# Gathered rows written first, VectorE for the last weight splits, norm factors on GpSimd, weights in blocks

## The chip, the cores and the metric

One core of one Trainium2 chip runs the whole program. The metric is the device time in microseconds, from launch to end; the median of three runs stands for a kernel. The core has TensorE (PE; PEld is its weight load), VectorE (DVE), ScalarE (ACT), GpSimd (POOL) and SyncE (SP). SP issues most transfers; GpSimd issues the gathers and scatters and most of the expert weights.

## The reference

A one-layer encoder block on 512 tokens plus 16 meta tokens, 1024 channels, all float32. Two attentions run side by side on the same normed input, their outputs are gated and merged, and a mixture of experts follows in which each expert picks its own 66 tokens:

```python
u = rms_norm(h, g_mix[layer])
z = jnp.einsum('bld,df->blf', u, w_in[layer])
qa, ka, va, qb, kb, vb, ga, gb = jnp.split(z, cut, axis=-1)
oa = diff_attention(...)                      # 8 heads, two softmaxes each
oa = rms_norm(oa, g_subln[layer]) * (1.0 - lam_init)
qh = axial_rope(rms_norm(qb, g_qnorm[layer]), ...)
kh = axial_rope(rms_norm(kb, g_knorm[layer]), ...)
ob = gqa_attention(qh, kh, vb)                # 8 query heads, 2 key heads
merged = sigmoid(ga) * (oa @ w_branch_a) + sigmoid(gb) * (ob @ w_branch_b)
h = h + merged @ w_out[layer]
un = rms_norm(h, g_ffn[layer])
aff = softmax(un @ w_router)                  # 16 experts
top_aff, top_idx = lax.top_k(swapaxes(aff, 1, 2), 66)
xs = un[top_idx]
y = (silu(xs @ w_gate) * (xs @ w_up)) @ w_down * top_aff
h = h.at[top_idx].add(y)
return rms_norm(h, g_final)[:, N_META:]
```

## The kernel before, in words

**Arithmetic.** float32 products are made of float32r halves: a tile is split into a high half (a ScalarE copy that rounds) and a low half (the difference, on VectorE or GpSimd; `hi_lo`, line 440), and a product is three matmuls: high by high, high by low, low by high.

**Projections.** All weights of the first part are taken as 76 column tiles of 1024 x 128 in a fixed order (`order`, line 514): for each of 8 heads of the first attention q, k, v; then the second attention's tiles mixed with the first gates and branch A; then 8 each of gb, yb (branch B) and wo (output projection). `load_weights` (465) brings a tile in from SP, three buffers deep (wraw); a row of it is 128 numbers, so each partition reads 8 runs of 512 bytes. `split_weights` (477) splits it in two parts; the low half goes to `spare_engine()` (444), which is GpSimd unless its planned queue is over 800 ns ahead. `project` (493) makes 24 matmuls for columns 0 to 255 and 24 for the other 272, splits the next tile meanwhile, and yields after matmuls 6, 12, 18 of each half and after the half's evacuation, so that other work can be put between.

**Order.** `Pace` (126) keeps a planned clock for each engine. TensorE and DMA instructions are issued in program order; ScalarE, VectorE and GpSimd instructions wait in a list and are issued by planned start and by `pace.prio` (lower goes first). The order on each engine is fixed at build time.

**Norm factors.** For the 8 heads of the first attention, the 8 queries and the 2 keys of the second, `add_norm` (739) and `norm` (746) sum squares with matmuls against `sel`, turn the sums so that they stand in 5 columns (tile cols5), and `rsqrt` (453) takes the reciprocal root on VectorE: a bit trick and three Newton steps, 11 instructions. For the heads and keys TensorE then spreads the factors over a row (`tr` of a broadcast column) and VectorE multiplies; for the queries the factors become scale and bias of the softmax (cols).

**Output projection and routing.** For d = 0 to 7 `project` makes wo's block d. `route(d)` (1307) adds it to h2T, splits the sum (hh, hl), squares it, and leaves its matmuls for router logits and square sums in `routed`; the loop of the next block issues one of them after each of its first yields:

```python
for n, _ in enumerate(g):
    if n < todo:
        routed.pop(0)()
```

Before the last block `split_piece(0)` (1266) splits the first quarter of expert 0's gate matrix, low half on GpSimd; quarters 1 and 2 follow after the routing probabilities.

**Rows.** `put_rows(t)` (1362) turns 88 tokens of h2T back into rows (t = 0 to 5; the last has 72 tokens and the 16 meta tokens, hence two transfers), copies them to SBUF, and sends them to acc in DRAM, where the experts' results are added later. When the norm factors rc are known, `send_rows` (1379) lets GpSimd write the factor into 4 more columns, and the same rows go to urow in DRAM (1028 columns), from which the experts gather. Rows 0, 1, 2, 4 and 5 use the three wraw buffers, row 3 one named ys. All of these transfers are issued by SP. Beside them VectorE finds each expert's 66 best tokens in 9 rounds (line 1437); `until(idxu)` (1468) plans for the indices; `gather(e)` (1472) takes a wraw buffer and reads the rows of expert e from urow by an indirect transfer of GpSimd.

**Experts.** 48 matrices of 2 MB stream through a ring of 8 buffers (`ring`, 1200, `load_mat`, 1211); the first (tiles named first, tags xa and xb) and the next seven are loaded by SP while wo and the routing run, the rest by GpSimd when VectorE has released a buffer. Each is split in four pieces by ScalarE (eh) and VectorE (el), and TensorE multiplies. Matrix 7 goes where mg_l was. The last expert's rows are added in SBUF, the final norm is made, and the output is written.

## Time and profile before

| What | Value |
|---|---|
| median of three runs | 1073.41 us (1071.48 to 1073.82) |
| the profiled execution, time | 1074.43 us |
| the profiled execution, span | 1072.7 us, mean granted clock 0.968 |
| PE busy | 969.4 us (90%) |
| DVE busy | 758.2 us (71%) |
| ACT busy | 630.8 us (59%) |
| POOL busy | 338.7 us (32%) |
| first attention, second attention, wo and routing, experts | about 30 to 305, 305 to 582, 670 to 752, 765 to 1045 us |

Every instruction stands under line 199, where the planner issues it, so the groups are told apart by their tiles: wl<-wraw,wh is the low half of a weight tile, cols the 5-column factors, hl the low half of h2T, row the rows, xs the gathered rows, raw the expert weights, eh and el the halves of a piece. Times in a timeline count from the first instruction. "[0.52 <-DVE hl]" behind an instruction means that its engine stood idle for 0.52 us before it, and that an instruction of VectorE that wrote hl ended that.

### The profile page before, as it was taken

Reading aid. Unit: us, or ns where it says so; the run is one execution under the profiler, and the core shown is the slowest. Engines: PE = TensorE matmul, PEld = TensorE weight load, DVE = VectorE, ACT = ScalarE, POOL = GpSimd, SP = SyncE. Lnnn points to the kernel's source line nnn. Section 1 sums busy time; section 2 is a strip of 40 time slices with the busy share of each in tenths; the row PEclk is TensorE's granted clock in tenths of the full one; section 3 lists DMA queues with packets and bytes.
Section 4 is the critical chain, followed back from the end, with each engine's and each line's share of the span. In section 5 each row is a group of like instructions: output and inputs, shape, how many; then the busy total and the mean of one; then the engine's idle time right before and its main releaser. Section 6 shows DMA issues by size and latency. Waiting matters only on the chain.

```text
span 1072.7 us, 18211 instructions
## 1 busy us (share of the span) xinstructions
PE 969.4 (90%) x6835; PEld 836.1 (78%) x6835; DVE 758.2 (71%) x1550; ACT 630.8 (59%) x1297; POOL 338.7 (32%) x306
## 2 busy tenths in 40 slices
PE   4799999999968999999999999985499999999984
PEld 4799998999958989999999999974256666666562
DVE  5367788887785677676656145566389999999885
ACT  5366666665745455555545433334288888888773
POOL 3232322322312322333223234432223333323153
PEclk9899999999989999999999999998699999999997
DMA  8544444443111222222222545915899999999964
GB/s 246 166 126 109 124 122 119 130 126 100 55 51 42 66 62 71 69 56 65 70 60 83 160 157 171 328 73 201 237 301 376 324 381 328 381 342 361 349 182 184
DMA packets 127502, 186.44 MB, mean 174 GB/s; under 512 B 6298, under 2 KB 84263, under 8 KB 127414
## 3 DMA queue, kind: packets, MB, share of 16 engines
q1 hardware_dynamic: 101046, 87.96, 27.5%
q0 software_dynamic: 25760, 95.16, 26.2%
q10 hardware_dynamic: 608, 2.16, 0.7%
q8 instruction: 54, 0.88, 0.3%
q14 instruction: 34, 0.28, 0.1%
HBM read 162.07 MB, written 10.76 MB: 161 GB/s over the span
## 4 chain that ended last, share of the span: by engine, by line
PE 57%; DVE 21%; ACT 9%; DMA 5%; issue 5%; SPq 1%; POOL 1%; POOLq 0%; ACTq 0%; DVEq 0%
PE pz L199 33%; PE psc L199 19%; PE ptr L199 5%; DVE sn L199 4%; DVE cols L199 3%; ACT sn L199 2%; DVE ls L199 2%; DVE pb L199 2%; SPq L199 1%; DVE wtl L199 1%; DMA raw<-in_w_down_dram 1%; DVE hl L199 1%; DVE nmb L199 1%; DVE ql L199 1%; DVE zb L199 1%
## 5 line engine op out<-in xcount | busy, mean ns | idle before, releaser
L199 POOL TENSOR_TENSOR wl<-wraw,wh 128x512 fp32r<-128x512 f32 x139 | 190.6, 1381 | 475.2 <-ACT wh L199 453.1
L199 PE MATMUL pz<-u_h,wh 128*128 128x256 f32 (+1 forms) x832 | 247.2, 297 | 5.4 <-ACT u_h L199 2.3
L199 PE MATMUL pz<-u_h,wl 128*128 128x256 f32 (+1 forms) x832 | 238.6, 287 | 1.1 <-POOL wl L199 1.1
L199 PE MATMUL pz<-u_l,wh 128*128 128x256 f32 (+1 forms) x832 | 238.4, 287 | 0.4 <-DVE u_l L199 0.4
L199 DVE TENSOR_TENSOR el<-raw,eh 128x1024 fp32r<-128x1024 f32 x180 | 214.0, 1229 | 6.0 <-ACT eh L199 4.9
L199 ACT CAST eh<-raw 128x1024 fp32r<-128x1024 f32 x180 | 182.0, 1049 | 23.5 <-PE pz L199 14.9
L199 PEld LDWEIGHTS pz<-u_h,wh 128*128 128x128 f32 x832 | 158.8, 191 | 8.3 <-DVE kbuf L199 2.7
L199 PEld LDWEIGHTS pz<-u_h,wl 128*128 128x128 f32 x832 | 158.5, 190 | 1.3 <-POOL wl L199 1.3
L199 PEld LDWEIGHTS pz<-u_l,wh 128*128 128x128 f32 x832 | 158.8, 191 | 0.6 <-DVE u_l L199 0.6
L199 PE MATMUL psc<-eh,xh 128*66 128x512 f32 (+1 forms) x272 | 105.0, 386 | 2.7 <-ACT hid L199 2.2
L199 ACT CAST wh<-wraw 128x512 fp32r<-128x512 f32 x152 | 91.0, 617 | 24.2 <-PE pz L199 10.9
L199 PE MATMUL psc<-el,xh 128*66 128x512 f32 (+1 forms) x272 | 104.1, 383 | 0.9 <-DVE el L199 0.9
L199 PE MATMUL psc<-eh,xl 128*66 128x512 f32 (+1 forms) x272 | 104.0, 382 | 0.0
L199 DVE TENSOR_TENSOR wtl<-ptr,wth 128x512 fp32r<-128x512 f32 (+1 forms) x72 | 45.9, 637 | 46.7 <-ACT wth L199 46.1
L199 ACT ACTIVATE sn<-sn,nm 128x528 f32<-128x528 f32 x64 | 47.1, 736 | 47.0 <-DVE nm L199 46.4
L199 PE MATMUL pz<-eh,hhl 128*66 128x512 f32 x224 | 70.7, 396 | 0.6 <-DVE hhl L199 0.6
L199 POOL DMA_INDIRECT acc<-ys,idxu x15 | 28.8, 1921 | 119.8 <-ACT ys L199 117.5
L199 ACT CAST wth<-ptr 128x512 fp32r<-128x512 f32 (+1 forms) x72 | 39.0, 542 | 46.0 <-PE ptr L199 45.5
L199 PEld LDWEIGHTS psc<-eh,xh 128*66 128x66 f32 x272 | 37.5, 138 | 25.4 <-ACT hid L199 3.2
L199 PEld LDWEIGHTS psc<-el,xh 128*66 128x66 f32 x272 | 37.3, 137 | 24.4 <-DVE el L199 1.4
L199 PEld LDWEIGHTS psc<-eh,xl 128*66 128x66 f32 x272 | 37.4, 138 | 21.9 <-issue 0.6
L199 DVE CUSTOM_DVE_ANT_0 sn<-psc,biases 128x528 f32<-128x528 f32 x64 | 44.3, 694 | 6.2 <-PE psc L199 6.2
(311 smaller groups left out, 2352.2 us busy)
## 6 DMA issues: line engine op xcount, KB each, us to landing
wraw<-in_w_in_dram SPq DMA_DIRECT2D x52, 512.0 KB
raw<-in_w_gate_dram POOLq DMA_DIRECT2D x13, 2048.0 KB, 18.5
raw<-in_w_down_dram POOLq DMA_DIRECT2D x13, 2048.0 KB, 15.4
raw<-in_w_up_dram POOLq DMA_DIRECT2D x13, 2048.0 KB, 20.4
biases<-in_c_bias_dram SPq DMA_DIRECT2D x8, 1056.0 KB
kbuf<-kbuf SPq DMA_DIRECT2D x32, 132.0 KB
wraw<-in_w_branch_a_dram SPq DMA_DIRECT2D x8, 512.0 KB
wraw<-in_w_branch_b_dram SPq DMA_DIRECT2D x8, 512.0 KB
```

Source lines behind the costliest of these rows:

```text
L199: op.fn(*op.args, **op.kw)
```

## The change

It has five parts. (1) The host lays w_in, w_branch_a, w_branch_b and w_out out as blocks of 128 partitions x 8 x 128, so that a tile's load reads 4 KB in one run for each partition. (2) `norm` calls a new `root`, five GpSimd instructions, in place of `rsqrt`; the four-wide router norm keeps `rsqrt`. (3) From the first yb tile on the low halves of weights go to VectorE, and the router matmuls left over from the block before are issued after the yields 1, 4 and 6. (4) No expert piece is split before or within the routing: the first two pieces get their high halves (`start_piece`) when the rows have been sent, and their low halves, with all of piece 2, on VectorE after the indices. (5) Rows go to urow at once, without factors; rows 4 and 5 have one tile in mg_l's place; the factors go in one GpSimd copy and three transfers of 16 bytes a row; then all rows go to acc.

```diff
+    def root(y, a, t):
+        nc.gpsimd.tensor_tensor(y, a, halfs[:, :a.shape[1]], op=OP.pow)
+        nc.gpsimd.tensor_mul(t, y, y)
+        nc.gpsimd.tensor_mul(t, t, a)
+        nc.gpsimd.tensor_scalar(t, t, -0.5, 1.5, op0=OP.mult, op1=OP.add)
+        nc.gpsimd.tensor_mul(y, y, t)
...
-            nc.sync.dma_start(raw, w[:, c0:c0 + P].rearrange("(c p) f -> p c f", p=P))
+            nc.sync.dma_start(raw, w_cols[stream[j]])
...
-                hi_lo(wh[:, b], wl[:, b], loaded[j][:, b], spare_engine())
+                hi_lo(wh[:, b], wl[:, b], loaded[j][:, b], nc.vector if j >= jof["yb", 0] else spare_engine())
...
+    nc.gpsimd.memset(halfs, -0.5)
...
-        rsqrt(y, a, t_, c[:, 3, :])
+        root(y, a, t_)
...
+    def start_piece(k):
+        hi, lo = [wk.tile([P, 1024], F32R, tag=tag, bufs=2, name=name) for tag, name in (("wh", "eh"), ("wl", "el"))]
+        prio, pace.prio = pace.prio, 2
+        nc.scalar.copy(hi, raws[0][k])
+        pace.prio = prio
+        return hi, lo
...
-            tags = spots[i if k else 1]
+            tags = spots[i]
...
-        hi_lo(hi, lo, src, nc.gpsimd if k < 3 or n in whole and i > 1 else None)
+        hi_lo(hi, lo, src, nc.gpsimd if n in whole and i > 1 else None)
...
-        if d == NC - 1:
-            split_piece(0)
...
-            if n < todo:
+            if n in (1, 4, 6)[:todo]:
                 routed.pop(0)()
...
     def put_rows(t):
-        row = (pc.tile([TQ, DX], F32, tag="ys", bufs=2, name="row") if t == 3 else
+        if t == 4:
+            rowq.append(pc.tile([TQ, 2, DX], F32, tag="mg_l", name="rowp"))
+        row = (rowq[4][:, t - 4] if t > 3 else pc.tile([TQ, DX], F32, tag="ys", bufs=2, name="row") if t == 3 else
                wk.tile([TQ, DX], F32, tag="wraw", bufs=3, name="row"))
...
-        send(acc, t, row, D)
-        rowq.append((t, row))
+        row = row[:, :D]
+        send(urow, t, row)
+        if t < 4:
+            rowq.append(row)
...
-    def send_rows():
-        for t, row in rowq:
-            nc.gpsimd.tensor_copy(row[:, D:], rc[:, t:t + 1].to_broadcast([TQ, DX - D]))
-            send(urow, t, row, DX)
-        rowq.clear()
+    def send_factors():
+        rc4 = pc.tile([TQ, NT, DX - D], F32, name="rc4")
+        nc.gpsimd.tensor_copy(rc4, rc.unsqueeze(2).to_broadcast([TQ, NT, DX - D]))
+        n = NT - 1
+        nc.sync.dma_start(urow[M:M + n * TQ, D:].rearrange("(t p) w -> p t w", p=TQ), rc4[:, :n])
+        send(urow, n, rc4[:, n], slice(D, DX))
...
-    split_piece(1)
-    split_piece(2)
...
-    send_rows()
     for t in range(3, NT):
         put_rows(t)
-        send_rows()
+    send_factors()
+    for t in range(NT):
+        send(acc, t, (rowq[t] if t < 4 else rowq[4][:, t - 4, :D]))
     load_mat(7, parts=2)
+    firsts = [start_piece(k) for k in range(2)]
...
     until(idxu)
+    for k, (hi, lo) in enumerate(firsts):
+        nc.vector.tensor_sub(lo, raws[0][k], hi.bitcast(F32))
+        pieces[k] = hi, lo
+    split_piece(2)
...
+def column_blocks(*mats):
+    wide = np.concatenate([m.reshape(NC, P, -1) for m in mats], axis=2)
+    return np.ascontiguousarray(wide.reshape(NC, P, -1, P).transpose(2, 1, 0, 3))
```

## Rows read from the trace of the kernel before

**Rows 1.** Busy time by stage; us, busy (instructions) of each engine, PEclk, DMA share, GB/s

```profile
100.00:200.00 100.00, 94.16 (x771) 91.85 (x770) 80.86 (x208) 60.48 (x165) 29.32 (x26) 1.00 0.43 118
...
640.00:660.00 20.00, 20.00 (x166) 20.00 (x166) 10.65 (x21) 7.24 (x15) 9.73 (x7) 1.00 0.65 208
...
860.00:960.00 100.00, 100.00 (x487) 60.77 (x486) 93.22 (x105) 84.28 (x104) 34.91 (x34) 1.00 1.03 360
```

**Rows 2.** Whom TensorE waited for, 100 to 300 us; total us, times, longest

```profile
PE pz L199 <- DVE cols L199: 4.5, 3, 1.5
PE psc L199 <- DVE nm L199: 4.3, 3, 1.4
```

**Rows 3.** The same, 300 to 400 us; and busy time, 312 to 321 us

```profile
PE pz L199 <- DVE cols L199: 5.2, 1, 5.2
...
312.00:321.00 9.00, 6.31 (x23) 4.99 (x24) 6.83 (x19) 2.49 (x8) 0.00 (x0) 0.50 0.06 18
```

**Rows 4.** Timeline of GpSimd and VectorE, 306 to 311 us

```profile
306.78 2.48 POOL L199 TENSOR_TENSOR wl<-wraw,wh 128x512 fp32r<-128x512 f32 x2 [12.35 <-DMA zp<-zb]
...
308.11 2.43 DVE L199 TENSOR_TENSOR cols<-cols 128x5 f32<-128x5 f32 x2
```

**Rows 5.** Whom TensorE waited for, 670 to 731 us; timeline of TensorE

```profile
PE psc L199 <- DVE hl L199: 6.4, 8, 2.0
...
730.88 0.30 PE L199 MATMUL psc<-hl,wr 128*16 128x272 f32 x1 [1.23 <-DVE hl L199]
```

**Rows 6.** Instructions that write hl, ns min/median/max; timeline of GpSimd

```profile
L199 DVE TENSOR_TENSOR hl<-h2T,hh x16: 425/755/2380, 673.8 to 730.4; 128x256 fp32r<-128x256 f32 x8, 128x272 fp32r<-128x272 f32 x8
...
719.17 2.36 POOL L199 TENSOR_TENSOR el<-first,eh 128x1024 fp32r<-128x1024 f32 x1 [4.74 <-ACT eh L199]
```

**Rows 7.** Busy time in three stretches around the last wo block

```profile
713.48:717.00 3.52, 3.52 (x30) 3.52 (x30) 2.44 (x4) 0.72 (x2) 0.95 (x1) 1.00 0.02 5
719.56:724.17 4.61, 2.09 (x15) 1.28 (x14) 3.32 (x3) 0.81 (x2) 1.97 (x1) 0.96 0.00 0
724.17:727.24 3.07, 3.07 (x16) 3.07 (x15) 0.85 (x2) 0.72 (x2) 0.00 (x0) 0.51 0.00 0
```

**Rows 8.** Timeline of VectorE, GpSimd and SP, 743 to 759 us

```profile
743.28 1.58 SPq L199 DMA_DIRECT2D acc<-row  x1
...
751.98 1.83 SPq L199 DMA_DIRECT2D urow<-row  x2
...
752.04 0.17 DVE L199 TENSOR_TENSOR idxu<-take,ptr 66x16 uint32<-66x16 f32 x1
...
758.27 1.03 POOL L199 DMA_INDIRECT xs<-urow,idxu  x1 [11.12 <-DMA urow<-row]
```

**Rows 9.** Transfers that touch xs, issue to landing

```profile
DMA to landing us min/median/max: 7.2/14.6/25.8
```

**Rows 10.** Groups of VectorE and GpSimd; busy us, mean ns, idle before

```profile
L199 DVE TENSOR_TENSOR cols<-cols 128x5 f32<-128x5 f32 x108 | 26.4, 246 | 2.0
...
L199 DVE TENSOR_SCALAR cols<-cols 128x5 int32<-128x5 int32 x18 | 9.7, 540 | 0.6
L199 DVE SCALAR_TENSOR_TENSOR cols<-cols 128x5 f32<-128x5 f32 x54 | 8.8, 164 | 1.4
...
L199 POOL TENSOR_TENSOR wl<-wraw,wh 128x512 fp32r<-128x512 f32 x139 | 190.6, 1381 | 475.2 <-ACT wh L199 453.1 <-DMA zp<-zb 14.9 <-PE ptr L199 3.0
...
L199 POOL CAST last<-idxu 66x1 f32<-66x1 uint32 x1 | 1.3, 1251 | 0.0
```

**Rows 11.** DMA queues of the page; whom TensorE waited for, 0 to 60 us

```profile
q1 hardware_dynamic: 101046, 87.96, 27.5%
q0 software_dynamic: 25760, 95.16, 26.2%
...
PE psc L199 <- DMA kbuf<-kbuf: 6.7, 1, 6.7
```

**Rows 12.** Whom GpSimd waited for, 760 to 1073 us

```profile
POOL raw L199 <- DVE el L199: 53.8, 13, 8.1
```

More of the change, by code (lines that the diff above doesn't have):

```diff
@@ L73, in keys @@
     step = ap.ap[0][0]
-    width = {"kbuf": L, "biases": 4 * L, "h2T": L, "xin": D, "pair": L, "obf": L, "hrow": D, "junk": D, "big": D, "first": D, "raw": D,
+    width = {"kbuf": L, "rowp": DX, "biases": 4 * L, "h2T": L, "xin": D, "pair": L, "obf": L, "hrow": D, "junk": D, "big": D, "first": D, "raw": D,
              "hid": FF // 2, "hhl": 2 * CAP, "xg": 4 * CAP}.get(kind, step)
@@ L292, in block_kernel @@
 @with_exitstack
-def block_kernel(ctx: ExitStack, tc: tile.TileContext, x, meta_tokens, g_mix, w_in,
+def block_kernel(ctx: ExitStack, tc: tile.TileContext, x, meta_tokens, g_mix, w_cols,
                  lambda_q1, lambda_k1, lambda_q2, lambda_k2, g_subln, g_qnorm, g_knorm,
-                 w_branch_a, w_branch_b, w_out, g_ffn, w_router, w_gate, w_up, w_down,
+                 g_ffn, w_router, w_gate, w_up, w_down,
                  g_final, c_bias, c_cos, c_sin, c_ident, c_sign, c_rev, out):
@@ L299, in block_kernel @@
     nc = Engines(pace, tc.nc)
[L300 to L301 removed]
+    nblocks = [C_GB // P + NC]
+    nblocks += [nblocks[0] + NC, nblocks[0] + 2 * NC]
     w_router, w_gate, w_up, w_down = w_router[0], w_gate[0], w_up[0], w_down[0]
@@ L331, in block_kernel @@
     rsx = {}
-    cols5 = [const.tile([P, 4, 5], F32, name=f"cols5{i}") for i in range(3)]
+    cols5 = [const.tile([P, 3, 5], F32, name=f"cols5{i}") for i in range(3)]
     sums5 = [const.tile([P, 2, 5], F32, name=f"sums5{i}") for i in range(2)]
@@ L515, in block_kernel @@
     for h in range(NH):
-        order += [("qa", w_in, C_QA + h * P), ("ka", w_in, C_KA + h * P), ("va", w_in, C_VA + h * P)]
-    cols_of = dict(q=("qb", w_in, C_QB), k=("kb", w_in, C_KB), v=("vb", w_in, C_VB))
+        order += [("qa", 0, C_QA + h * P), ("ka", 0, C_KA + h * P), ("va", 0, C_VA + h * P)]
+    cols_of = dict(q=("qb", 0, C_QB), k=("kb", 0, C_KB), v=("vb", 0, C_VB))
     order += [cols_of[c] for c in K["o7"]]
     for h in range(NH):
-        cols_of = dict(q=("qb", w_in, C_QB + (h + 1) * P), k=("kb", w_in, C_KB + P), v=("vb", w_in, C_VB + P),
-                       g=("ga", w_in, C_GA + h * P), y=("ya", wa, h * P))
+        cols_of = dict(q=("qb", 0, C_QB + (h + 1) * P), k=("kb", 0, C_KB + P), v=("vb", 0, C_VB + P),
+                       g=("ga", 0, C_GA + h * P), y=("ya", nblocks[0], h * P))
         order += [cols_of[c] for c in (K[("b0", "b1", "bn")[min(h, 2)]] if h + 1 < NH else "gy")]
     for d in range(NC):
-        order.append(("gb", w_in, C_GB + d * P))
+        order.append(("gb", 0, C_GB + d * P))
     for d in range(NC):
-        order.append(("yb", wb, d * P))
+        order.append(("yb", nblocks[1], d * P))
     for d in range(NC):
-        order.append(("wo", wo, d * P))
-    stream += [(w, c) for _, w, c in order]
+        order.append(("wo", nblocks[2], d * P))
+    stream += [w + c // P for _, w, c in order]
     jof = {}
@@ L540, in block_kernel @@
     sel = pb.tile([P, 2, P], F32R, name="sel")
+    halfs = pb.tile([P, 5], F32, name="halfs")
     vmeta = [pb.tile([P, P], F32R, name=f"vm{i}") for i in range(2)]
@@ L1369, in put_rows, with send @@
             nc.scalar.copy(row[:, 512 * b:512 * b + 512], pt[:TQ, :])
-        send(acc, t, row, D)
-        rowq.append((t, row))
-    def send(dst, t, row, w):
+        row = row[:, :D]
+        send(urow, t, row)
+        if t < 4:
+            rowq.append(row)
+    def send(dst, t, row, cs=slice(0, D)):
         n = TQ if t + 1 < NT else S - t * TQ
-        nc.sync.dma_start(dst[M + t * TQ:M + t * TQ + n, :], row[:n, :w])
+        nc.sync.dma_start(dst[M + t * TQ:M + t * TQ + n, cs], row[:n])
         if n < TQ:
-            nc.sync.dma_start(dst[:M, :], row[n:, :w])
-    def send_rows():
-        for t, row in rowq:
-            nc.gpsimd.tensor_copy(row[:, D:], rc[:, t:t + 1].to_broadcast([TQ, DX - D]))
-            send(urow, t, row, DX)
-        rowq.clear()
+            nc.sync.dma_start(dst[:M, cs], row[n:])
+    def send_factors():
[4 more added lines that the diff above has]
+        send(urow, n, rc4[:, n], slice(D, DX))
     pace.prio = 1
@@ L1750 @@
     arrays, args = {}, []
-    feed = [(n, inputs[n]) for n in _INS] + list(shape_constants().items())
+    given = dict(inputs)
+    given["w_in"] = column_blocks(*(np.asarray(inputs[n])[0] for n in ("w_in", "w_branch_a", "w_branch_b", "w_out")))
+    feed = [(n, given[n]) for n in _INS] + list(shape_constants().items())
     for name, value in feed:
```

5 lines of the change are left out of this document (1 added, 4 removed).

## The prediction

> **What bounds the kernel now.** I read the profile by stages first, since the busy shares of the whole span hide three different limits. In the attention stretches TensorE is busy 94 of 100 us beside VectorE at 81; in the weight projections it is busy all the time (20.00 of 20); in the experts too (100.00 of 100), there with the DMA engines full [rows 1]. So time can only be gained where TensorE stands still. Next I read, stretch by stretch, whom TensorE waited for.
>
> In a stretch of six attention heads it waited 4.5 us for the norm factors (cols) and 4.3 us for the softmax maxima (nm), both VectorE work [rows 2]. Where attention passes from the first kind of head to the second one wait for the factors took 5.2 us, and behind it the granted clock was 0.50, the lower level (1.2 GHz), for about 9 us [rows 3]. There VectorE was at the Newton steps while GpSimd ran weight splits: two 5-column products took 2.43 us together [rows 4].
>
> In the output projection (wo) TensorE waited for the low half of h2T, hl: 6.4 us in 8 waits, the longest 2.0 [rows 5]. The hl subtraction takes 0.43 us at best and 2.38 at worst; the worst began just after GpSimd began a 2.36 us split of the first expert weights [rows 6]. The last of the eight blocks then costs twice: 4.61 us with 15 matmuls, and 3.07 us with 16 at the lower clock, against 30 in 3.52 before [rows 7].
>
> Last the chain of waits after routing: the indices (idxu) are ready at 752.04 + 0.17 = 752.21, the first gather starts at 758.27, since GpSimd waits for the last urow writes, issued from 751.98 on behind the acc writes of the same rows [rows 8]. The gathered rows land 7.2 us later, the shortest of 16 [rows 9]. TensorE has nothing to do meanwhile.
>
> **The change, part by part.** The profiled execution took 1074.43 us (span 1072.7 and 1.7 around it), 1.0 above the median of the runs, 1073.41; I sum against 1074.43 and take the 1.0 off at the end.
>
> *a) Output projection.* The router sums of the block before are issued after matmuls 12 and 30 of the next block instead of 6 and 12, and low halves of weights go to VectorE, so GpSimd no longer runs beside hl. The second half of a block now has 18 matmuls more, about 18 x 0.117 = 2.1 us, to get its hl ready; the wait it replaces was some 0.5. Of the 6.4 us, 2.0 lie in the last block and 1.23 behind it, where no matmul is left to cover them [rows 5]: 6.4 - 2.0 - 1.2 = 3.2 gained. In the last block the first-expert split is gone too: 15 matmuls at 3.52 / 30 = 0.117 us are 1.76 instead of 4.61, and 16 are 1.88 instead of 3.07 [rows 7]. Sum 3.2 + 2.9 + 1.2 = 7.3; the 1.2 at the end stays. The subtractions that VectorE takes over cost about 1.4 us for each block of some 6; it is busy 10.65 of 20 us in the stage before [rows 1], and gets back what hl lost to GpSimd. I cost them at nothing; without that cover they would put 1.4 us on each of 16 blocks.
>
> *b) First gather.* acc writes leave the path: urow rows are sent as they are made, rows 4 and 5 have a place of their own, and no ScalarE or GpSimd split stands between. Three factor transfers of 16 bytes a row follow, then the seven acc writes, then the seventh expert load. By SP's rows a write takes 0.9 to 1.6 us to issue [rows 8]; an estimate from these: rows 3 to 5 and the three factor writes, from about 740 on, are all issued by 747, some 5 us before the indices. Gained at most 758.27 - 752.21 less a hand-over of 0.3 = 5.8 us. Two things are new. The first three gathers take the buffers of rows 0 to 2, which the acc writes now read last, so they wait for these; behind the first gather stand the other two and the loads of the eighth expert matrix on GpSimd's queue. And the gather lands beside acc writes: the median of all 16 is 14.6 us [rows 9]. I take 8.5, nearest to this same gather's 7.2, so 5.8 - 1.3 = 4.5, with ends 5.8 and -1.6. The low halves of the first pieces (three subtractions on VectorE) lie under this wait of 7 us and more; the seventh load is needed two experts later.
>
> A rule speaks against b. The Trainium skill, DMA: Bandwidth & Descriptors, section Specifications, says that transfers under 512 bytes make the DMA engine read, modify and write. No row here shows 16-byte writes to DRAM; by that rule the 528 factor rows are the slow part, and the gather waits for them as it did for the last rows (second rival).
>
> *c) Norm factors.* 18 norms lose 11 VectorE instructions each: 26.4 + 9.7 + 8.8 us in three groups [rows 10], and 18 scalings at the 0.16 of the third, 47.8 us in all, 2.7 a norm. GpSimd gets 5. No row shows pow. Upper end: the longest one-column GpSimd instruction, 1251 ns; lower end: a two-input one of 512 columns takes 1381 ns, 2.7 a column, so that five columns are next to nothing and the instruction's fixed part, at least the 0.1 us of a short one, remains (an estimate) [rows 10]. Between 0.5 and 6.3 us a norm I take 1.5: five columns lie near the lower end, and pow counts for three. The factors then come sooner than now, and VectorE has 2.7 us more in the burst in which nm and cols are late. Of the 4.5 + 4.3 us I count half, 4, because GpSimd's own splits stand ahead in its queue and the planner reorders everything; the new constant tile and the narrower factor tile cost nothing, since they are set before the first head. At the passage between head kinds 2 of the 5.2, one split still ahead of the factors. Ends: all of it with the clock (14 + 4 = 18 gained), or the loss of the third rival.
>
> *d) Weights in blocks.* 76 loads of 512 KB become 128 runs of 4 KB for 1024 of 512 bytes. The queue with these loads moved 87.96 MB in 27.5% of the engines' time, the other 95.16 in 26.2% [rows 11]: 17% slower a byte, all packets together. Past the start the loads run three tiles ahead, which hides them. At the start the rows of x and the kbuf moves, for which TensorE waited 6.7 us [rows 11], queue behind weight loads of about 2 us: I take 1 us, ends 0 and 2.5.
>
> Sum: 7.3 + 4.5 + 6 + 1 = 18.8; 1074.43 - 18.8 = 1055.6, less 1.0: **1055 us** rounded.
>
> **The rivals.**
> *Attention gives nothing*: the planner puts other work where VectorE is freed, and the waits move. For it: TensorE is already at 94 of 100. Against: the burst around the factors is what is late. Time 1055 + 6 = 1061.
> *The gather still waits*, for the factor packets or the acc writes that hold its buffers: b is worth 0, 1055 + 4.5 = 1059.5.
> *The experts give it back*: their stage moves 360 GB/s at a DMA share of 1.03 [rows 1]; if the loads set its pace, the 7.3 + 4.5 gained before it are lost: 1067. The same page and section of the Trainium skill give about 358 GB/s as the limit of HBM for a core; by that rule this stage is at the limit, and ends when the bytes are in. Against: TensorE is busy 100.00 of 100 there, and 13 loads waited for VectorE to release their buffers, 53.8 us in all [rows 12], so the compute sets the pace.
> *Slower*: GpSimd's five instructions take the 1.25 us of the upper end. The planner prices them below 0.1 us each and puts the transposes of the factors in TensorE's fixed order too early; 8 + 2 norms have such transposes. Each then stalls by 6.3 - 2.7 = 3.6 us more than now, 36 in all, against a + b + d = 12.8: 1073.4 + 23 = 1097. It decides from (2.7 + 1.28) / 5 = 0.8 us an instruction.
>
> **How the numbers follow.** Chances: forecast 0.55, attention nothing 0.18, gather waits 0.13, experts 0.08, slower 0.06. The range goes down to 1043 (c at its full 18) and up to 1067, which takes in the first three rivals. About 0.2% (2.1 us) is what a measurement of this kernel can tell from no change. Faster by more than that: all but the slower rival and a little of the experts', 0.93; slower 0.05; the rest 0.02.
>
> **What would show it.** TensorE's waits for hl down to one of 1.2 us and no lower clock at the end of wo; the first gather within 1 us of idxu, its rows landing 7 to 9 us later; VectorE without the 5-column steps (about 48 us less busy, plus some 20 of splits), five GpSimd instructions a norm of well under 0.8 us; fewer waits for cols and nm. I am wrong if TensorE's waits for the factors grow, if the gather starts at a landing of factors or acc, or if the experts' stretch from first gather to end gets longer than now.

## The result and the profile after

The changed kernel takes 1066.64 us (median), the kernel before 1072.24 in the runs shown beside it: 0.9939 of the time, 95% interval 0.9924 to 0.9954. One of its six runs took 4508 us; the ratio leaves that run out, and the median of the other five is 1065.83. So it takes 5.6 to 6.4 us less; the forecast was 18.8. The two profiled executions lie further apart than the medians, 1074.43 and 1065.83, spans 1072.7 and 1064.1. Their 8.6 us can be followed stretch by stretch, so the accounts below are made on them.

Cut at events that both traces have, the span falls into pieces (us): *start*, until VectorE reads the first scores; *heads*, from there until it reads the last bias; *rest*, the second attention and its projections, up to the first matmul of wo; *wo*, from there to idxf (the sums, the routing, the top lists); *idx*, idxf to idxu; *gap*, idxu to the start of the first gather (idxf and idxu by the starts of their instructions); *land*, that start to TensorE's first use of the rows; *end*, all behind. All kernels that were run are here; the times are medians. The pieces are those of the one execution that was profiled, which can lie up to 4 us from the median (g_free 1060.31, d_undone 1068.56), so they need not add up to the time. Among kernels with the same edits of a piece, heads and rest agree within 1 us and wo within 0.1, but start scatters over 2 us and end over 3. Where the intervals of two times overlap, the text goes by the pieces.

| kernel | time | start | heads | rest | wo | idx | gap | land | end |
|---|---|---|---|---|---|---|---|---|---|
| before | 1072.24 | 51.2 | 252.8 | 365.9 | 80.2 | 1.9 | 6.3 | 7.3 | 307.1 |
| after | 1066.64 | 50.7 | 248.6 | 372.1 | 71.4 | 5.7 | 1.2 | 8.8 | 305.6 |
| c_undone | 1064.11 | 50.0 | 252.9 | 366.1 | 71.4 | 6.4 | 1.2 | 8.8 | 307.0 |
| c_q_undone | 1068.79 | 50.3 | 250.6 | 370.8 | 71.4 | 6.5 | 1.2 | 8.5 | 306.9 |
| c_heads_only | 1063.89 | 50.1 | 250.3 | 369.1 | 71.3 | 4.9 | 1.2 | 7.8 | 307.4 |
| c_q_scaled | 1059.15 | 51.9 | 248.6 | 367.4 | 71.3 | 5.9 | 1.2 | 6.0 | 307.8 |
| c_priced | 1059.24 | 50.8 | 248.3 | 366.7 | 71.4 | 6.0 | 1.2 | 5.5 | 307.1 |
| g_load7 | 1062.68 | 50.8 | 249.3 | 372.6 | 71.3 | 5.6 | 1.2 | 5.8 | 305.6 |
| g_subs | 1062.11 | 51.0 | 248.4 | 372.0 | 71.4 | 5.7 | 1.2 | 4.3 | 304.7 |
| g_free | 1064.27 | 50.5 | 248.6 | 371.9 | 71.4 | 1.9 | 1.1 | 8.1 | 305.0 |
| g_free_load7 | 1061.66 | 49.8 | 248.7 | 372.2 | 71.4 | 1.9 | 1.1 | 6.7 | 306.5 |
| g_quiet | 1062.20 | 50.9 | 249.0 | 372.4 | 71.4 | 2.0 | 1.1 | 7.3 | 306.1 |
| g_acc_last | 1065.21 | 51.8 | 249.1 | 372.5 | 71.4 | 1.9 | 1.1 | 4.3 | 311.5 |
| a_split_undone | 1062.66 | 50.0 | 249.3 | 372.3 | 71.4 | 4.9 | 1.2 | 4.6 | 307.1 |
| a_pos_undone | 1065.80 | 51.7 | 248.8 | 372.4 | 72.6 | 6.3 | 1.2 | 7.8 | 306.5 |
| a_both_undone | 1069.71 | 51.0 | 249.4 | 372.7 | 76.4 | 6.0 | 1.1 | 4.6 | 307.4 |
| d_undone | 1064.74 | 52.5 | 249.3 | 372.6 | 71.4 | 6.1 | 1.2 | 6.0 | 307.7 |
| best | 1054.96 | 50.6 | 246.9 | 366.6 | 71.4 | 1.9 | 1.1 | 7.7 | 306.6 |
| best2 | 1055.35 | 49.8 | 248.0 | 365.7 | 71.4 | 1.9 | 1.2 | 4.1 | 311.9 |
| best3 | 1060.53 | 50.8 | 249.3 | 368.5 | 71.4 | 2.0 | 1.1 | 9.0 | 307.3 |

From before to after: start -0.5, heads -4.2, rest +6.2, wo -8.8, the three pieces of the gather together +0.2 (15.5 to 15.7), end -1.5; the sum is -8.6. Of the four parts of the change, a (wo) gave more than forecast, b (the gather) gave nothing, c (heads and rest) lost 2.0, and d (start) cannot be told from nothing.

Heads and rest have to be read together, since the plan moved work across the cut between them. These are heads and rest before, then heads and rest after:

```profile
51.20:304.00 252.80, 240.97 (x1957) 235.18 (x1957) 195.96 (x516) 157.55 (x427) 69.87 (x59) 0.99 0.41 112
304.00:669.90 365.90, 346.59 (x2781) 337.87 (x2780) 221.10 (x546) 178.77 (x448) 118.53 (x88) 0.98 0.29 85
...
50.70:299.30 248.60, 238.72 (x1939) 233.29 (x1939) 179.21 (x438) 156.11 (x423) 80.40 (x93) 1.00 0.40 113
299.30:671.40 372.10, 348.03 (x2799) 339.81 (x2797) 204.26 (x445) 179.38 (x452) 117.76 (x128) 0.98 0.28 85
```

After the change heads have 18 matmuls fewer and the rest has 18 more, by an estimate at the prediction's 0.117 us each 2.1 us. TensorE's idle time in heads falls from 11.8 to 9.9 us, in the rest it grows from 19.3 to 24.1. So some 2 of the 4.2 us are waits that went, and the others are work that stands behind the cut now.

The page of the changed kernel: busy time and the two large DMA queues.

```profile
PE 965.7 (91%) x6835; PEld 835.1 (78%) x6835; DVE 724.8 (68%) x1386; ACT 630.5 (59%) x1297; POOL 325.6 (31%) x358
...
q1 hardware_dynamic: 33517, 87.96, 26.6%
q0 software_dynamic: 25760, 95.16, 26.0%
```

The blocks cut q1's packets to a third at the same bytes, but its share only from 27.5 to 26.6% [rows 11]. TensorE's waits, as in [rows 2], [rows 3] and [rows 5], in 100 to 300, 300 to 400, 400 to 583 and 668 to 740 us:

```profile
PE pz L199 <- POOL cols L199: 4.7, 4, 1.2
...
PE pz L199 <- POOL cols L199: 6.2, 4, 3.1
...
PE ptr L199 <- DVE pb L199: 7.8, 6, 1.4
...
PE psc L199 <- DVE hl L199: 1.2, 1, 1.2
```

In the heads the waits for nm are gone and those for the factors stay. In wo one wait for hl is left of eight. The third line is new in size: the softmax rows pb of the second attention cost 3.2 us there before. At the passage the granted clock is at the lower level for as long as before, 10.2 us, only earlier. The first row of the following fence is the second attention, TensorE 56.98 of 60; the other two are the passage's stretch at the lower clock, after and before.

```profile
400.00:460.00 60.00, 56.98 (x468) 55.84 (x467) 37.72 (x84) 32.22 (x87) 21.14 (x24) 1.00 0.22 63
...
309.00:319.20 10.20, 6.05 (x25) 5.18 (x26) 3.69 (x8) 2.84 (x7) 2.04 (x5) 0.50 0.01 3
...
310.80:321.00 10.20, 6.31 (x23) 4.99 (x24) 7.86 (x25) 2.49 (x8) 0.00 (x0) 0.50 0.15 45
```

The instructions that write the factors and hl (ns min/median/max) answer to [rows 10] and [rows 6]:

```profile
L199 POOL TENSOR_TENSOR cols<-cols x54: 187/196/652, 102.5 to 537.2; 128x5 f32<-128x5 f32 x54
...
L199 POOL TENSOR_TENSOR cols<-cols,halfs x18: 1166/1167/1619, 100.0 to 535.1; 128x5 f32<-128x5 f32 x18
...
L199 DVE TENSOR_TENSOR hl<-h2T,hh x16: 425/430/442, 675.7 to 723.1; 128x256 fp32r<-128x256 f32 x8, 128x272 fp32r<-128x272 f32 x8
```

A power of five columns takes 1.17 us, three products 0.2 each and the scaling about 0.2: some 1.95 us a norm where 1.5 was forecast. hl no longer takes 2.38 us anywhere.

Two timelines show where the rest went. First one query norm of the second attention, VectorE, GpSimd and TensorE:

```profile
445.09 0.21 DVE L199 TENSOR_SCALAR cols<-ptr 128x4 f32<-128x4 f32 x2
...
445.37 1.17 POOL L199 TENSOR_TENSOR cols<-cols,halfs 128x5 f32<-128x5 f32 x1 [1.85 <-DVE cols L199]
...
447.46 0.20 POOL L199 TENSOR_TENSOR cols<-cols 128x5 f32<-128x5 f32 x1
447.61 2.51 POOL L199 TENSOR_TENSOR wl<-wraw,wh 128x512 fp32r<-128x512 f32 x2
447.69 1.31 DVE L199 TENSOR_SCALAR cols<-cols 128x5 f32<-128x5 f32 x2 [1.18 <-POOL cols L199]
...
449.10 1.32 DVE L199 TENSOR_SCALAR pb<-pb,ls 128x528 f32<-128x528 f32 x1
...
450.56 0.74 PE L199 MATMUL ptr<-ident,pb 128*128 128x128 f32 x5 [1.40 <-DVE pb L199]
```

VectorE's two scalings of the factors stand directly behind the root in its order. It waits 1.18 us for GpSimd, then takes 1.31 us for two scalings of 0.16, beside a 1.25 us split that GpSimd began 0.08 us before; pb, behind them, is 1.4 us late for TensorE. Second, the first gather:

```profile
743.41 0.22 DVE L199 COPY lists<-ptr 66x64 f32<-66x64 f32 x1 [0.35 <-PE ptr L199]
...
747.89 0.17 DVE L199 TENSOR_TENSOR take<-lists,ptr 66x16 f32<-66x16 f32 x1 [4.26 <-DMA acc<-row]
...
748.46 0.17 DVE L199 TENSOR_TENSOR idxu<-take,ptr 66x16 uint32<-66x16 f32 x1
748.55 3.66 DVE L199 TENSOR_TENSOR el<-first,eh 128x1024 fp32r<-128x1024 f32 x3
749.67 2.16 POOL L199 DMA_INDIRECT xs<-urow,idxu  x1 [19.49 <-DMA acc<-rowp]
...
751.08 0.40 SPq L199 DMA_DIRECT2D raw<-in_w_up_dram  x1
...
758.45 1.11 PE L199 MATMUL ptr<-ident,xs 66*128 66x66 f32 x8 [14.31 <-DMA xs<-urow,idxu]
```

The wait for the urow writes is gone [rows 8]. In its place VectorE waits 4.26 us with the small tile `take`, whose buffer (tag "ys") held row 3 of h until acc's write of it had landed; the gather's issue takes 2.16 us where it took 1.03; and TensorE has the rows 8.8 us after its start, not 7.3. The acc writes are all but over by then: the DMA engines' busy share is 0.13 during the issue and 0.95 behind it, with the load under way:

```profile
749.67:751.83 2.16, 0.00 (x0) 0.00 (x0) 2.07 (x3) 1.04 (x1) 2.16 (x1) 0.50 0.13 47
751.83:758.45 6.62, 0.00 (x0) 0.03 (x1) 0.38 (x1) 0.00 (x0) 3.80 (x5) 0.50 0.95 255
```

### The profile page after: what moved, and what is told of

It reads as the page before. It is cut to its first block, busy times and chain, and to the rows that moved or that the text cites. A ratio compares the mean times of both kernels' runs of the same rounds, so it can differ in the third digit from the quotient of the medians.

```text
span 1064.1 us, 18086 instructions
## 1 busy us (share of the span) xinstructions
PE 965.7 (91%) x6835; PEld 835.1 (78%) x6835; DVE 724.8 (68%) x1386; ACT 630.5 (59%) x1297; POOL 325.6 (31%) x358
## 3 DMA queue, kind: packets, MB, share of 16 engines
q1 hardware_dynamic: 33517, 87.96, 26.6%
q0 software_dynamic: 25760, 95.16, 26.0%
q10 hardware_dynamic: 608, 2.16, 0.6%
## 4 chain that ended last, share of the span: by engine, by line
PE 52%; DVE 4%; DMA 3%; ACT 2%; POOL 2%; issue 2%; SPq 1%; POOLq 0%; ACTq 0%; DVEq 0%
PE pz L199 31%; PE psc L199 17%; PE ptr L199 4%; POOL cols L199 1%; DMA raw<-in_w_down_dram 1%; DMA xs<-urow,idxu 1%; DVE pb L199 1%; DVE cols L199 1%; POOL big L199 1%; SPq L199 1%; DMA acc<-rowp 1%; ACT big L199 0%; DMA xrow<-in_x_dram 0%; DMA gfc<-in_g_ffn_dram 0%; DVE hrow L199 0%
## 5 line engine op out<-in xcount | busy, mean ns | idle before, releaser
L199 POOL TENSOR_TENSOR wl<-wraw,wh 128x512 fp32r<-128x512 f32 x108 | 145.3, 1352 | 359.5 <-ACT wh L199 352.2
L199 DVE TENSOR_TENSOR wl<-wraw,wh 128x512 fp32r<-128x512 f32 x44 | 32.9, 753 | 31.5 <-ACT wh L199 30.5
```

The source lines that it names most:

```text
L199: op.fn(*op.args, **op.kw)
```

## The experiments

**Norm factors (c).** First the whole part is undone, then the query norms alone:

```diff
-    cols5 = [const.tile([P, 3, 5], F32, ...
+    cols5 = [const.tile([P, 4, 5], F32, ...                      # both
-        root(y, a, t_)
+        rsqrt(y, a, t_, c[:, 3, :])                              # c_undone
+        root(...) if spread is not None else rsqrt(...)          # c_q_undone
```

> The changed kernel with the norm factors of all 18 norms back on VectorE (Newton steps). Theory: the root on GpSimd gained about 4 us in the first heads (last bias read 304.0 -> 299.3 us) and lost about 6 from there to the end of attention, because VectorE, in order, stands behind GpSimd's 1.17 us instruction. Then the two cancel: last bias read back at about 303.5, wo's first matmul at 669 to 671, total 1063 to 1067 against 1066.6. Rival: the loss after 300 us comes from the reordering that any edit of the plan brings, not from the root; then the 6 stay lost and the heads' 4 are lost too: 1070 to 1072.

Measured: 1064.11 us, ratio 0.9921 (0.9902 to 0.994). Heads 252.9, rest 366.1, both within 0.2 of before. So the root, with the plan that follows from it, explains both, the 4.3 by which heads shrank and the 6.0 by which the rest grew. Eleven of the kernels in the table have the norms of the changed kernel; their heads and rest together take 620.4 to 622.1 us, 621.3 in the mean, against 619.0 here. By these traces part c as it was made costs 2.3 us; the intervals of the two times overlap.

> The changed kernel with only the 8 query norms of the second attention back on VectorE; the 8 head norms and 2 key norms stay on GpSimd. Theory (VectorE stands behind GpSimd there): the heads keep their 4 us, TensorE's waits for pb from 400 to 583 us go from 7.8 back to about 3, and 4 to 5 us are gained: 1061 to 1063. Rival (reordering, or the passage alone): the waits stay at 7 to 8 us, 1065 to 1068.

Measured: 1068.79, ratio 0.997 (0.9956 to 0.9984). A miss: the waits for pb fell to 3.2 us as expected, but the heads lost 2.0 of their 4.2 and the rest gained only 1.3. From the last bias read to the first maxima of the second attention there are 23.6 us here (324.5 - 300.9), 22.9 in the changed kernel and 14.7 before; so the place where the planner sets the passage's work moved too.

Next the stand of VectorE is attacked directly, by moving the two scalings, and by telling the planner the measured prices (it takes 71 ns for any 5-column GpSimd instruction):

```diff
-                nc.vector.tensor_scalar(cols[:, 0, :], c[:, 1, :], sc, ...)
-                nc.vector.tensor_scalar(cols[:, 1, :], c[:, 1, :], -sc, ...)
+                nc.gpsimd.tensor_scalar(...)                     # c_q_scaled: both
+        if self.eng == "gpsimd" and n == 5:                      # c_priced: in Op.price
+            return 1170.0 if self.kw.get("op") == OP.pow else 190.0
```

> The changed kernel with the two scalings of a query norm's factors on GpSimd too, so that VectorE issues nothing behind the root before the next maxima need it. Theory: VectorE's 5 waits of 1.2 us and its scaling of 1.24 us go (it stood 2.3 us a norm); 3 to 5 us gained, 1062 to 1064, unless the later factors make the exponentials wait. Rival (reordering): 1065 to 1068.

> The changed kernel with one edit to the planner: it prices a 5-column GpSimd instruction at 190 ns and the power at 1170 ns (the trace's 187 to 197 and 1167) instead of 71. Theory: it then puts other VectorE work ahead of what needs the factors and places the transposes of the factors later; TensorE's waits for cols (4.7 us in 100 to 300, 6.2 in 300 to 400) and for pb (7.8) fall by a third or more: 1060 to 1064. Rival (order makes no difference, the factors are simply late): 1066 to 1068.

Measured: 1059.15 (0.9878, 0.9861 to 0.9894) and 1059.24 (0.988, 0.9863 to 0.9897). TensorE's waits for pb in 400 to 583 us, first with the scalings moved, then with the prices:

```profile
PE ptr L199 <- DVE pb L199: 1.9, 6, 0.8
```

```profile
PE ptr L201 <- DVE pb L201: 1.2, 3, 0.8
```

Heads and rest take 616.0 and 615.0 us, 5.3 and 6.3 less than the 621.3, and the waits for pb fall by 5.9 and 6.6 from the 7.8. That is the cause as far as it is shown: VectorE, which works in order, stood behind an instruction on GpSimd that the planner held for sixteen times shorter than it is. Against it stands c_q_undone, in which 4.6 us of these waits went and nothing was gained. All these edits change the plan too, and no run parts the two. (Both also had 2.8 and 3.3 us less landing, by chance; see g_subs.)

```diff
+        rsqrt(...) if sums is None else root(y, a, t_)          # c_heads_only
```

> The changed kernel with the root on GpSimd only in the 8 head norms of the first attention; the 2 key norms and 8 query norms of the second are on VectorE as before. Theory: the heads' 4 us stay (248.6 us from the first scores to the last bias read), and the passage (14.7 us from the last bias read to the first maxima of the second attention before, 22.9 after, 23.6 with only the queries undone) was stretched by the key norms' roots, so it is back at 15 and the rest of attention at 366 to 367 instead of 372.1: 1060 to 1062.5 against 1066.6. Rival (the last head norms' own roots, or the order of the plan, stretch the passage): passage 20 to 24, rest 370 to 372, 1065 to 1068.

Measured: 1063.89 (0.991, 0.9893 to 0.9926). The rival: the passage takes 22.8 us (323.2 - 300.4) with no root of its own, the rest 369.1. What lengthens it is open: a last head norm's root or the plan's order. Only whole plans could be compared here, since every edit of c moves both. The length alone is not what costs: the passage takes 23 to 24 us in c_priced and best too, and the rest 366.7 and 366.6. Heads and rest of c_heads_only:

```profile
50.10:300.40 250.30, 238.57 (x1939) 232.98 (x1938) 181.06 (x447) 156.11 (x423) 77.50 (x88) 1.00 0.39 113
300.40:669.50 369.10, 350.06 (x2800) 340.76 (x2799) 225.21 (x545) 179.84 (x452) 99.44 (x82) 0.98 0.28 86
```

TensorE is idle for 11.7 us in heads and 19.0 in the rest, as before (11.8 and 19.3), and both together take 619.4 us against c_undone's 619.0. So roots on GpSimd in the head norms alone gained nothing here; the shorter heads are the 18 matmuls that stand behind the cut.

**The first gather (b).** One edit each: the seventh expert load, in one piece, behind the gathers on GpSimd's queue, and the first two subtractions of expert pieces behind the first gather's issue (the diffs are shortened):

```diff
-        eng = nc.gpsimd if n > 7 else nc.sync            # g_load7
+        eng = nc.gpsimd if n > 6 else nc.sync
-    load_mat(7, parts=2)
     gather(2)
-    load_rest()
+    load_mat(7)
```

```diff
-        nc.vector.tensor_sub(lo, raws[0][k], hi.bitcast(F32))      # g_subs
     gather(0)
+    nc.gpsimd.memset(zero, 0.0)
+        nc.vector.scalar_tensor_tensor(lo, raws[0][k], zero, hi, op0=OP.add, op1=OP.subtract)
```

> The changed kernel with the seventh expert load (up matrix of the second expert, 1 MB first half on SP's queue at 751.08 us, 1.4 us after the first gather began) moved behind the three gathers on GpSimd's queue. Theory: its packets stood ahead of the gather's, whose descriptors were only written by 751.83; the rows then land 5 to 6.5 us after the gather's start instead of 8.7, and 2 to 3 us are gained: 1063.5 to 1065 against 1066.6. Rival 1 (the 8.7 us come from the slow issue beside VectorE's subtractions, 2.16 us, or from the gather itself): landing stays at 8 to 9, 1066 to 1068. Rival 2: the later load is missed by the second expert, 1067 to 1070.

> The changed kernel with one edit: the first two subtractions of expert pieces wait until the first gather is issued. Rows, acc writes and the seventh load stay as they are. Theory: the gather's issue of 2.16 us is GpSimd waiting for the end of a VectorE subtraction (749.67 + 2.16 = the end of the second one + 0.8), and that delay lets the seventh load, issued 1.4 us after the gather's start, go ahead of its rows; then the issue is 1.05, the rows land 4.7 to 6 us after the start instead of 8.7, and the total is 1062 to 1064. Rival (load and rows share the queues in any order): landing 7.5 to 9, 1065.5 to 1067.5.

Measured: 1062.68 (0.9909, 0.989 to 0.9928) and 1062.11 (0.9904, 0.9872 to 0.9935). The timeline of g_subs:

```profile
749.74 1.06 POOL L199 DMA_INDIRECT xs<-urow,idxu  x1 [19.57 <-DMA acc<-rowp]
...
750.96 2.48 DVE L199 SCALAR_TENSOR_TENSOR el<-first,zero,eh 128x1024 fp32r<-128x1024 f32 x2 [2.25 <-POOL zero L199]
751.11 1.99 POOL L199 DMA_INDIRECT xs<-urow,idxu  x1 [0.18 <-issue]
751.60 0.40 SPq L199 DMA_DIRECT2D raw<-in_w_up_dram  x1
...
754.05 1.11 PE L199 MATMUL ptr<-ident,xs 66*128 66x66 f32 x8 [9.92 <-DMA xs<-urow,idxu]
```

With VectorE quiet the first issue is 1.06 us; the second, beside the subtractions, is 1.99. The load comes 0.8 us after the first issue has ended, and the rows land 4.3 us after the start. Across the runs with these acc writes the order decides: where the load's issue begins 0.5 to 1.0 us before the gather's issue ends (after, c_undone, c_q_undone, a_pos_undone, c_heads_only) the rows come 5.6 to 6.7 us after that end; where it begins at most 0.3 before it or later (c_q_scaled, d_undone, c_priced, a_split_undone, a_both_undone, g_subs), 3.3 to 3.8. In g_load7 the issue still takes 2.16 us, but with no load ahead of them the rows come 3.7 us after its end and 5.8 after its start: 3.0 us are the load's. So the changed kernel loses 4.5 us by a start that falls beside a subtraction: 1.1 in the issue, the rest behind the load that slips ahead.

Now the buffers. Rows 0 to 3 go to mg_l's place and rows 4 and 5 to weight buffers, so that neither `take` nor the first gather needs a buffer of an acc write:

```diff
+        if t == 0:                           # g_free
+            rowq.append(pc.tile([TQ, 4, DX], F32, tag="mg_l", name="rowp"))
+        row = rowq[0][:, t] if t < 4 else wk.tile([TQ, DX], F32, tag="wraw", bufs=3, name="row")
```

> The changed kernel with rows 0 to 3 of h in mg_l's place and rows 4 and 5 in two of the three weight buffers, so that neither the lists of the indices nor the first gather need a buffer that an acc write still reads. Theory: the 4.26 us that VectorE waited for acc's write of row 3 go, the indices are ready at about 744.5 and the first gather starts within 1.3 us of them; it then runs beside the acc writes (DMA share 0.7), so its rows land 7 to 10 us later; xs is there at 753 to 756 against 758.45, and the total is 1062 to 1064.5. Rival (the gather waits for the 16-byte factor writes, which stand on the same queues): indices at 744.5, gather still at 747 or later: 1065 to 1067.

> Both edits of the two runs before together. Theory: the two are independent; indices at 744.5, gather within 1.3 us, landing in 6 to 8 us, total 1060.5 to 1063. Rival (load and gather are not in each other's way, only the acc writes are): the same as with the rows moved alone, within 0.7 us.

> The version with rows 0 to 3 in mg_l's place and the seventh load behind the gathers, and besides the first two subtractions of expert pieces made to wait until the first gather is issued (they read a zero that GpSimd writes behind it). Theory: GpSimd's issue of 2.2 us and its 1.1 us from indices to start are long because VectorE subtracts at the same time; issue back to about 1.05, start within 0.5 us of idxu, rows 1 to 1.7 us sooner after idxu than without (idxu to xs 7.8 us there): 1060 to 1061. Rival (GpSimd's issue has another cause): issue 2.2 as before, and the later subtractions cost 0 to 1.5: 1061.5 to 1063.

Measured: 1064.27 (0.9927, 0.9908 to 0.9946), with g_load7's edit too 1061.66 (0.9904, 0.9884 to 0.9924), with both others 1062.20 (0.9899, 0.9874 to 0.9925). The timeline of g_free:

```profile
743.74 0.17 DVE L199 TENSOR_TENSOR take<-lists,ptr 66x16 f32<-66x16 f32 x1 [0.54 <-PE ptr L199]
...
744.30 0.17 DVE L199 TENSOR_TENSOR idxu<-take,ptr 66x16 uint32<-66x16 f32 x1
...
745.42 2.24 POOL L199 DMA_INDIRECT xs<-urow,idxu  x1 [15.69 <-DMA acc<-rowp]
```

idx is 1.9 us again, so row 3's buffer was the 3.8 us. The gather starts 1.1 us after idxu starts, 0.95 after it ends, as in every changed kernel (0.95 to 1.04): it waits for no factor packet; the last of these are issued by 739.5, 6 us before it. But now it runs beside acc writes and lands in 8.1 us, without the load 6.7. g_quiet met its rival's time: the issue is back to 1.05 us and nothing is gained, since the rows wait for the acc writes ahead of them, as the next run shows. It starts from g_quiet and puts most acc writes behind the gathers, and the seventh load behind the fourth gather:

```diff
-    for t in range(NT):                      # g_acc_last
-        send(acc, t, ...)
+    for t in (4, 5):
+        send(acc, t, rowq[t - 3])
     gather(2)
-    load_mat(7)
+    for t in range(4):
+        nc.gpsimd.dma_start(acc[M + t * TQ:M + t * TQ + TQ, :], rowq[0][:, t, :D])
...
     gather(3)
+    load_mat(7)
```

> The version with rows 0 to 3 in mg_l's place, the seventh load behind the gathers and quiet subtractions (idxu to xs 8.3 us, 1062.2), with the acc writes of rows 0 to 3 moved behind the three gathers on GpSimd's queue, and the seventh load behind the fourth gather. Theory: there the rows landed 7.3 us after the gather's start because 7 acc writes (DMA share 0.7) were under way; with three of them they land in 4.7 to 5.5: xs 2 to 2.5 us sooner, 1059.5 to 1061. Rival (the landing has a floor that acc does not set): 7 us again, 1061.5 to 1064.

Measured: 1065.21 (0.9918, 0.9886 to 0.9949). The landing is 4.3 us, 3.0 less than in g_quiet, but the end takes 311.5 instead of 306: the load that needs mg_l's place now waits for the late acc writes (5.2 us in best2, below), and the experts give back more than was won.

**Output projection (a)** and **blocks (d)**, each undone in the changed kernel:

```diff
+    hi_lo(wh[:, b], wl[:, b], loaded[j][:, b], spare_engine())   # a_split_undone
+            if n < todo:                                         # a_pos_undone; both: a_both_undone
+    nc.sync.dma_start(raw, w_cols[:, P * stream[j]:P * stream[j] + P].rearrange(...))   # d_undone
```

> The changed kernel with the low halves of the weights of yb and wo given to GpSimd again where it is free, and nothing else undone. Theory (GpSimd's splits beside VectorE are what made hl late): hl takes up to 2.4 us again, TensorE waits for it 3 to 6 us in wo, wo grows by 3 to 6: total 1069.5 to 1072.5 against 1066.6. Rival (the later places of the router sums alone cover hl): no waits for hl but the last one, 1066 to 1067.5.

> The changed kernel with the router sums of a block issued after 6 and 12 matmuls of the next block again instead of 12 and 30. Theory (both parts are needed; a low half alone is some 0.43 us without GpSimd but ScalarE's and VectorE's other work stands ahead): hl waits of 0.5 us or less in each of 7 blocks, 1 to 3.5 us: 1067.5 to 1070. Rival (without GpSimd beside it hl is early enough): 1066 to 1067.

> The changed kernel with both parts undone that each alone showed no wait for hl: low halves of yb's and wo's weights on GpSimd where it is free, and the router sums after 6 and 12 matmuls. Theory (each part alone covers the other): only now hl is late again, TensorE waits 3 to 6 us for it between wo's start and the last sums, where each alone showed 1.2 to 1.7; wo's start to idxu 80 to 83 us against 77.1. Total 1066 to 1072, depending on how the gather falls. Rival (what helped was only that the first expert pieces no longer run on ScalarE and GpSimd): waits of at most 2 us, stage 77 to 78.5.

Measured: 1062.66 (0.9899, 0.9876 to 0.9922), 1065.80 (0.9926, 0.9902 to 0.995) and 1069.71 (0.9969, 0.9952 to 0.9986). hl of a_split_undone, then TensorE's wait for it in a_both_undone:

```profile
L199 DVE TENSOR_TENSOR hl<-h2T,hh x16: 425/444/1281, 675.5 to 723.3; 128x256 fp32r<-128x256 f32 x8, 128x272 fp32r<-128x272 f32 x8
```

```profile
PE psc L199 <- DVE hl L199: 4.4, 7, 1.2
```

With GpSimd's splits back hl is late at times (1.28 us), but the later places of the sums hide it: wo 71.4. With the early places alone wo is 72.6. Only both together bring seven waits back, wo 76.4. Each half covers for the other. 3.8 us to the 80.2 of before are left. They lie in the eight blocks, since from the last block's matmul to idxf 21 us pass in all three kernels. The blocks before, in a_both_undone and after:

```profile
669.90:729.40 59.50, 53.81 (x420) 50.98 (x418) 32.19 (x46) 20.54 (x47) 21.31 (x15) 0.97 0.54 183
...
673.10:728.70 55.60, 51.97 (x419) 49.51 (x418) 30.24 (x46) 19.59 (x46) 18.93 (x14) 1.00 0.52 195
...
671.40:722.20 50.80, 50.80 (x420) 50.00 (x418) 27.59 (x60) 19.82 (x46) 0.00 (x0) 1.00 0.57 207
```

Before, the clock fell within the last block [rows 7]; in a_both_undone the granted clock is 1.00 over all of them. Of the edits that touch the blocks only the moved expert pieces were never put back, and their place, the last block, is where the clock fell; that they are worth the 3.8 us is so by elimination, not by a run of its own. a_split_undone is faster than the changed kernel mostly by its gather, which landed in 4.6.

> The changed kernel with the weights kept as columns of one wide matrix, loaded in 512-byte runs again instead of blocks of 4 KB. Theory (prediction: blocks are worth 1 us at the start, and their loads are hidden after it): the first scores 0.5 us later (51.2 against 50.7), total 1067 to 1068. Rival 1 (blocks are worth more, since the stages of wo and of the two attentions wait for loads): 1069 or more. Rival 2 (nothing): 1066 to 1067.

Measured: 1064.74 (0.9925, 0.9903 to 0.9946), no difference from the changed kernel's 0.9939 that the intervals allow. The start is 52.5, and with blocks 49.8 to 51.9 in the other 18 kernels, so its 0.5 us lies inside the scatter.

**Together.** *best* is c_q_scaled, c_priced and g_quiet in one; *best2* adds g_acc_last; *best3* is best with roots only in the head norms.

> All that helped, together: GpSimd's real prices in the planner, the query factors scaled on GpSimd, rows 0 to 3 in mg_l's place, the seventh load behind the gathers, the first subtractions behind the first gather. Theory: the attention edits (7.4 each alone, partly the same wait: some 8 together) and the gather edits (5 to 6) lie on different stretches and add, except that the priced version had its gather rows land in 5.5 us already: 1066.6 - 8 - 4 = 1054 to 1056. Rival (the planner's order moves again and takes part of it back): 1057 to 1060.

> The best version so far (1054.96) with the same move of acc writes and load. Theory: 2 to 2.5 us less, 1052 to 1053.5. Rival: 1054.5 to 1056.5, the later acc writes and load given back by the first experts.

> The best version (1054.96) with the same choice: roots on GpSimd in the 8 head norms alone, real prices, rows 0 to 3 in mg_l's place, the seventh load behind the gathers, quiet subtractions. Theory: the rest of attention was 366.6 there with all roots on GpSimd and would be 366 with none, so no difference within 1 us: 1054 to 1056. Rival (the roots of the second attention hide work that the real prices then place well): 1057 to 1060.

Measured: 1054.96 (0.9828, 0.9805 to 0.9852), 1055.35 (0.9833, 0.9803 to 0.9863), 1060.53 (0.9874, 0.9857 to 0.989). best beats both kernels: the one before by 18 us (1073.40 in the runs beside it), the changed one by 12. best2 does what g_acc_last did. In its timeline the seventh load waits 5.2 us for the acc writes, and of TensorE's waits after 740 us the one for expert pieces is 2.8 us where the changed kernel has 0.9:

```profile
752.39 0.94 POOL L201 DMA_DIRECT2D raw<-in_w_up_dram  x1 [5.22 <-DMA acc<-rowp]
```

```profile
PE ptr L201 <- DMA xs<-urow,idxu: 5.9, 1, 5.9
...
PE psc L201 <- DVE el L201: 2.8, 6, 0.7
```

best3 lost 4.3 us of attention (617.8 against 613.5): with true prices the roots of the second attention, and the scalings that went back to VectorE with them, do pay on GpSimd, in this plan.

## Why the prediction was wrong

Of the 18.8 us that were forecast the two traces show 8.6. Part a gave 8.8 for 7.3, b lost 0.2 for a gain of 4.5, c lost 2.0 for a gain of 6, d gave 0.5 for 1, and the experts 1.5 that were not in the sum and lie within their scatter. The first two rivals, each priced alone, came true together: without c's 6 and b's 4.5 the sum is 8.3. That it is so near 8.6 is chance, since what a gave too much and what c lost about cancel.

*a)* Right in its mechanism, and 1.5 us too small. Waits for hl fell from 6.4 us in eight to one of 1.2, as said. The term that was too small is the 3.2 for the waits: a_both_undone and the changed kernel differ by 5.0 us, since besides the waits (4.4 to 1.2, which is the 3.2) TensorE is busy for 1.2 us less in the blocks. The 2.9 + 1.2 of the last block came as 3.8, by elimination. That both halves were needed, as the text assumed, is not so.

*b)* The step that failed is the wait for a buffer. "The first three gathers take the buffers of rows 0 to 2 ... so they wait for these" looked for the held buffer on the gather; it was on the index list, one step earlier, in the tag that row 3 shares: 3.8 us. The hand-over, put at 0.3 us behind the end of idxu, is 1.0: another 0.7. These are all but 0.2 of the 4.7 us between forecast and result. "I take 8.5" for the landing came out right, 8.65, and that is luck: it was taken from acc writes beside the gather, which were all but over, while the subtractions that were costed at nothing "under this wait" delayed the gather, and the seventh load went ahead of its rows. In the other versions TensorE has the rows 4.1 to 9.0 us after the start. The 16-byte writes, the second rival, cost nothing here, issued 5 us and more before the gather. The Trainium skill, DMA: Bandwidth & Descriptors, Specifications, has such writes read and modify first; no wait of these runs shows it.

*c)* The 4 us in the heads came in number only (4.2): about 2 us are waits that went, and the others are work that moved behind the cut. "The factors then come sooner than now" is wrong: GpSimd is busy 1.95 us a norm for the 1.5 of the text, and TensorE's waits for the factors grew from 4.5 to 4.7 us and at the passage, where "2 of the 5.2" were to go, from 5.2 to 6.2. That was one of the text's own signs of being wrong. Above all, the second attention does not stand in the sum at all: the text counted what VectorE no longer issues, and did not ask what stands behind the root on VectorE. There the waits for pb grew from 3.2 to 7.8 us. Its slower rival had the right mechanism, a price "below 0.1 us" against a real one above, but laid it on TensorE's transposes with a threshold of 0.8 us an instruction as an average. The average is 0.39; one instruction of 1.17 was enough, at another engine. With the prices and the scalings mended heads and rest take 613.5 instead of c_undone's 619.0: 5.5, close to the forecast 6, though not where it was forecast.

*d)* 0.5 us for 1, not to be told from nothing. The queue was also less slow than the text had it: 27.5% for 87.96 MB against 26.2% for 95.16 is 14% slower a byte, not 17.

The experts kept what came before them: their end is 305.6 us for 307.1, and 304.7 to 307.8 in all versions that leave the loads in time. The third rival becomes true where a load comes late (g_acc_last, best2). The experts' loads ran at 361 and 356 GB/s from 800 to 860 and 860 to 960 us in the changed kernel. The Trainium skill (same page and section) gives about 358 GB/s as HBM's limit for a core; the trace agrees, and it fits a stage with no room to catch up a late load.

## What to carry to other kernels

When work moves to another engine, list what stands behind its result on the engine that it left, and give the planner the measured price of each moved instruction before judging the move. Count the work on both sides of a cut before calling a shorter piece a gain: a planner moves work across it. For a chain that ends in a gather, follow every buffer of every small tile in the chain, not only the gather's own, and look at which other transfer is issued within a microsecond of it. An early start into full queues buys less than its time, and a write that is put off passes its delay on to the load that takes its place.

## What the runs showed of the hardware

A GpSimd power of 128x5 takes 1.17 us, a product of that size 0.20 (medians).

GpSimd's issue of an indirect gather takes 1.03 to 1.06 us with VectorE idle and 1.97 to 2.24 when it begins within a series of 1.22 us VectorE subtractions. The long ones end 0.83 to 0.93 us after the end of a subtraction (in the changed kernel the second one runs from 749.68 to 750.90, the issue until 751.83), as if the issue got its turn only between two of them. Where it begins 0.22 us before one of them ends it takes 1.15 (a_split_undone, a_both_undone), but 0.18 before, in g_free, it misses that end and takes 2.24. The second gathers of a_split_undone and a_both_undone begin within 0.01 us of the start of a subtraction and take 0.97 beside it. So an overlap alone does not lengthen the issue. The Trainium skill, SBUF — State Buffer, section SBUF: two separate sides, has GpSimd and a VectorE instruction with two SBUF inputs share a port pair that the first of them holds for its whole instruction, this against GpSimd instructions that read SBUF; the delayed issues agree. It tells of halted descriptor writing for VectorE's 2-port modes alone; what of the gather's issue waits here is not shown.

Between the end of idxu on VectorE and the start of the gather's issue on GpSimd lie 0.95 to 1.04 us in all 19 changed kernels.

A 1 MB load issued 0.5 to 1.0 us before the end of a gather's issue puts off its 66 rows by some 2 to 3 us (first use 5.6 to 6.7 us behind that end, against 3.3 to 3.8; 3.7 in g_load7, without the load).
